# Keys and queries by block products over the whole depth, with raw weights laid out and loaded by block

## The chip, the cores and the metric

The kernel runs on one core of a Trainium2 chip. The metric is the device time of one execution in microseconds (us); lower is better. Times are compared as medians of several executions. A core has TensorE (PE, with its weight loads shown as PEld), VectorE (DVE), ScalarE (ACT), GpSimd (POOL) and SyncE (SP), each with its own queue of instructions in order; DMA transfers are started from SP, ACT and POOL.

## The reference

One inference step of a two-layer trunk on 576 tokens: a prompt of 512 and eight samples of eight. Layer 0 is a gated short convolution; layer 1 is an mLSTM block with four heads of 512. What matters here is how layer 1 gets its keys and queries, and what it does with them:

```python
xm, z = jnp.split(h @ w_in, 2, axis=-1)
xc, new_buf = causal_dwconv(xm, conv_buf, conv_w)
xc = jax.nn.silu(xc + conv_b)
q = xc @ w_q                      # (576 x 2048) @ (2048 x 2048)
k = xc @ w_k
v = xm @ w_v
...
# per head and chunk of 64 tokens (8 for the samples)
S = jnp.einsum('bhid,bhjd->bhij', qj, kj) * jnp.exp(logD - m_row[..., None])
num = w_inter[..., None] * jnp.einsum('bhid,bhde->bhie', qj, C) + jnp.einsum('bhij,bhje->bhie', S, vj)
den = w_inter * jnp.einsum('bhid,bhd->bhi', qj, n) + jnp.sum(S, axis=-1)
C_new = decay[..., None, None] * C + jnp.einsum('bhjd,bhje->bhde', kw, vj)
```

Inputs and outputs are float32. `C` is the matrix memory, given for the eight samples (the old states) and zero for the prompt.

## The kernel before

**Products.** Data lie with features on the 128 partitions and the 576 tokens along the free axis. Each float32 operand is split in a high part, which TensorE takes as it is, and a low rest, and a product is three matmuls: high weight x high data, high x low, low x high. Weights are split in the kernel: `parts_of` copies the raw weights to the high part on ACT (L264) and subtracts on DVE (L265), in tiles of 512 columns (four buffers) or 256 (two buffers). A split tile serves 4 (or 2) blocks of 128 x 128.

**Block products.** Where two k-tiles of the input meet two tiles of the output and the tokens are taken as two halves of 288, `block_pair` (L330) forms a 2 x 2 block product with seven products instead of eight: sums and differences of the data (the "forms", made once by `forms` and kept) meet sums of the weight blocks a11, a12, a21, a22 (made on DVE for each step: L298, L299 and L350). The seven products go to three PSUM banks, called p1, p5 and p6, one after the other: a11, s1, s2, a12, a21, s2 again, a22; results are added up from the banks by ACT and DVE.

**The stage.** Keys and queries are made in 16 steps, heads in the order 3, 0, 1, 2 and four steps to a head. A step makes 128 key rows (`k`) and 128 query rows (`q`) for all tokens, from 16 k-tiles of `xc`, thus eight pairs of k-tiles. Six pairs go by block products (7 x 6 x 3 = 126 matmuls of 288 columns, L345) and the last four k-tiles plainly (`plain`, L433: 4 x 2 outputs x 2 halves x 3 = 48). The very first step, `gemm_first`, does four pairs by block and eight k-tiles plainly, since the forms of pairs 4 and 5 are still in the making. The raw weights of a step are four loads of 512 KB (`wr`, L320, issued by SP), asked for at the end of the step before by `block_weights`, which also makes the sums.

**What runs between.** `run` takes a piece of work from a list at marked places between products: transposes of the finished keys for storage (L768, L769), scores, gates. `drip` takes one from a slower list: `meet` (L909) multiplies a piece of an old state, loaded as two `c` tiles of 512 KB into two buffers, with the queries (`query_state`, L857). After eight pieces of a head the product is copied into a tile `qc`, which stays in one of the slots of 128 x 576 that hold nearly all data (`N_SLOT`, 70 of them) until `sample_numerators` (L1305) uses it, far behind. Only heads 3, 0 and 1 do so here; head 2 follows later.

**The end of the stage.** The last step ends with `next_stage`: it loads layer 1's eight input tiles `x` again, runs what is left in the list, and normalises them for the z branch (`second_norm`: L902 on DVE, then a split of each with L166 on ACT and L167 on DVE). The z tiles follow, with weights from chunk 192 on.

The code is written in the order in which each engine's queue gets its instructions, up to a scheduler that moves instructions a little by their estimated readiness; waits between engines are semaphores. An engine that waits holds all that stands behind it in its queue.

## Time and profile before

| | us |
|---|---|
| median of 3 runs (lowest, highest) | 1635.63 (1635.1, 1638.68) |
| profiled execution, its own time | 1636.74 |
| its span | 1634.9 |
| PE busy | 1610.5 |
| DVE busy | 1117.4 |
| ACT busy | 807.0 |
| stage of keys and queries, steps 2 to 15 | about 839 to 1236 |

The mean granted clock of TensorE in this execution is 0.994 of full speed. The profiled execution's time is its span and 1.84 us around it. Busy time is the union of an engine's instructions; matmuls overlap, so PE at 99% says that some matmul is always in flight. Group rows give line, engine, operation, output<-input, shapes and count, then busy time, mean ns of one, and the idle time of the engine just before them with what ended it. DMA rows give size and the median time from issue to landing.

### The profile page before, as it was taken

How to read it: one execution, taken by the hardware profiler on the slowest of the kernel's cores; microseconds unless marked ns; L12 is line 12 of the kernel's file. 1: busy time of each engine (PE TensorE's matmuls, PEld its weight loads, DVE VectorE, ACT ScalarE, POOL GpSimd, SP SyncE). 2: the span in 40 equal slices, each digit the busy share in tenths (PEclk: the TensorE clock that was granted, in tenths of full speed). 3: DMA queues.
4: the chain of work that ended last, by engine and by line, in shares of the span. 5: the costliest groups of instructions: out<-in, count | busy, mean ns of one | idle time of the engine just before them, and what ended most of it. 6: DMA issues, size and time to landing. Idle time of an engine off the chain costs nothing. (4 is left out here: it accounts for less than half of the span.)

```text
span 1634.9 us, 31031 instructions
## 1 busy us (share of the span) xinstructions
PE 1610.5 (99%) x11981; PEld 1540.3 (94%) x11981; DVE 1117.4 (68%) x2124; ACT 807.0 (49%) x1622; POOL 139.3 (9%) x263
## 2 busy tenths in 40 slices
PE   9999999999999999999999999999999998999998
PEld 9999999999999999999999998999997798999997
DVE  7988988886336985655865555445458578688765
ACT  5566666654233554444644444344345556555421
POOL 1111111110000000000011010010112000000000
PEclk9999999999999999999999999999999999999999
DMA  6477676754332434443533555455467898998992
GB/s 222 110 168 176 167 166 171 168 146 145 122 126 87 144 109 141 128 143 124 181 110 117 171 161 170 157 178 158 156 203 272 293 313 318 342 352 297 359 336 101
DMA packets 118052, 306.85 MB, mean 188 GB/s; under 512 B 12912, under 2 KB 29168, under 8 KB 117904
## 3 DMA queue, kind: packets, MB, share of 16 engines
q1 hardware_dynamic: 94480, 272.86, 50.0%
q0 software_dynamic: 8064, 14.68, 6.0%
q10 hardware_dynamic: 15360, 17.32, 3.1%
q8 instruction: 94, 1.54, 0.4%
q14 instruction: 54, 0.44, 0.1%
HBM read 244.29 MB, written 60.52 MB: 186 GB/s over the span
## 5 line engine op out<-in xcount | busy, mean ns | idle before, releaser
L345 PE MATMUL p<-hi,wh 128*128 128x288 f32 x1540 | 453.7, 296 | 1.7 <-ACT wh L264 1.0
L345 PE MATMUL p<-lo,wh 128*128 128x288 f32 x1540 | 452.6, 295 | 0.0
L345 PE MATMUL p<-hi,wl 128*128 128x288 f32 x1540 | 451.0, 295 | 0.2 <-DVE wl L265 0.2
L345 PEld LDWEIGHTS p<-hi,wh 128*128 128x128 f32 x1540 | 288.3, 188 | 12.8 <-DVE ws L350 6.6
L345 PEld LDWEIGHTS p<-lo,wh 128*128 128x128 f32 x1540 | 289.0, 188 | 0.0
L345 PEld LDWEIGHTS p<-hi,wl 128*128 128x128 f32 x1540 | 288.1, 188 | 0.6 <-DVE wl L265 0.6
L264 ACT CAST wh<-wr 128x512 fp32r<-128x512 f32 x298 | 171.4, 578 | 213.9 <-PE p L345 121.1
L265 DVE TENSOR_TENSOR wl<-wr,wh 128x512 fp32r<-128x512 f32 x298 | 184.9, 634 | 91.7 <-ACT wh L264 90.5
L235 PE MATMUL acc<-hi,wh 128*128 128x256 f32 (+1 forms) x1072 | 232.8, 298 | 2.5 <-ACT num L1302 1.2
L235 PE MATMUL acc<-lo,wh 128*128 128x256 f32 (+1 forms) x1072 | 231.3, 297 | 0.0
L235 PE MATMUL acc<-hi,wl 128*128 128x256 f32 (+1 forms) x1072 | 231.1, 297 | 0.0
L264 ACT CAST wh<-ws 128x512 fp32r<-128x512 f32 (+1 forms) x201 | 114.9, 573 | 195.2 <-PE p L345 121.9
L215 ACT CAST wh<-wr 128x512 fp32r<-128x512 f32 x170 | 105.0, 619 | 197.6 <-PE acc L235 149.5
L235 PEld LDWEIGHTS acc<-hi,wh 128*128 128x128 f32 x1072 | 180.1, 190 | 9.6 <-issue 3.9
L216 DVE TENSOR_TENSOR wl<-wr,wh 128x512 fp32r<-128x512 f32 x170 | 116.4, 688 | 102.4 <-ACT wh L215 90.6
L235 PEld LDWEIGHTS acc<-lo,wh 128*128 128x128 f32 x1072 | 179.8, 190 | 1.8 <-issue 1.7
L235 PEld LDWEIGHTS acc<-hi,wl 128*128 128x128 f32 x1072 | 179.7, 190 | 0.8 <-issue 0.7
L265 DVE TENSOR_TENSOR wl<-ws,wh 128x512 fp32r<-128x512 f32 (+1 forms) x201 | 125.4, 629 | 74.7 <-ACT wh L264 74.2
L433 PE MATMUL p<-hi,wh 128*128 128x288 f32 x496 | 109.2, 300 | 0.0
L433 PE MATMUL p<-hi,wl 128*128 128x288 f32 x496 | 107.8, 295 | 0.0
L433 PE MATMUL p<-lo,wh 128*128 128x288 f32 x496 | 106.6, 295 | 0.0
L1236 DVE SCALAR_TENSOR_TENSOR c<-c,cols,r 128x512 f32<-128x512 f32 x128 | 90.7, 741 | 16.5 <-PE r L1235 13.9
(385 smaller groups left out, 2569.0 us busy)
## 6 DMA issues: line engine op xcount, KB each, us to landing
wr<-wts SPq DMA_DIRECT2D x222, 512.0 KB, 3.6
c<-cs SPq DMA_DIRECT2D x128, 512.0 KB, 6.0
cs_out<-c SPq DMA_DIRECT2D x64, 512.0 KB, 7.0
ws<-wts SPq DMA_DIRECT2D x28, 256.0 KB, 4.3
ws<-wts POOLq DMA_DIRECT2D x28, 256.0 KB, 4.8
wr<-wts POOLq DMA_DIRECT2D x28, 256.0 KB, 4.2
x<-xcs SPq DMA_DIRECT2D x20, 288.0 KB, 4.3
x<-xT SPq DMA_DIRECT2D x16, 288.0 KB, 4.2
```

Source lines behind the costliest of these rows:

```text
L215: last_act[0] = nc.scalar.copy(hi, raw[:, 4 * i:4 * i + 4, :]).ins
L216: nc.vector.tensor_tensor(lo, raw[:, 4 * i:4 * i + 4, :], hi.bitcast(F32), ALU.subtract)
L235: nc.tensor.matmul(acc[:, o:o + j - i], a[:, k % 4, :], x[:, i:j], start=(first and k == 0 and p == 0), stop=(last and k == 7 and p == 2))
L264: last_act[0] = nc.scalar.copy(hi, src).ins
L265: nc.vector.tensor_tensor(lo, src, hi.bitcast(F32), ALU.subtract)
L345: nc.tensor.matmul(bank_, a[:, j, :], x, start=(start and n + j + i == 0), stop=(n == len(groups) - 1 and j == len(g) - 1 and i == 2), ski ...
L433: nc.tensor.matmul(b, a[:, k % 4, :], x[:, t:t + HT], start=bool(start) and k == 0 and i == 0, stop=(k == n - 1 and i == 2), skip_group_ch ...
L1236: ins = nc.vector.scalar_tensor_tensor(ct[:, j, :], ct[:, j, :], dec[:, o + j:o + j + 1], r, ALU.mult, ALU.add).ins
```

## The change

- Steps 0 and 1 multiply as before. While they run, the forms of the last two k-pairs are made too (`mixed_load(6)` and `(7)`), from `xc` tiles loaded again.
- Steps 2 to 15 use a new function `eight_pair`: all eight pairs by block products, 7 x 8 x 3 = 168 matmuls of 288 columns, every weight split 512 columns wide (the 256-wide buffers are gone). Banks and order of the seven products are as before; results go straight to `k` and `q` without the plain part's additions.
- The host lays out these steps' raw weights so that each load of 512 KB holds one block (a11, a12, a21 or a22) of all eight pairs. The loads for the next step are issued inside the step, block by block in the order a11, a21, a22, a12, after products 3, 4, 5 and 7, when the step's own tile comes free. The next step's first sums (a21 + a22, `eight_sums`) stand after product 7.
- `qc` of each head is stored to DRAM from ACT's queue (`qcs`, 128 x 513) and fetched again when that head's numerators are at their second tile. The second norm's row scale `rb` is stored to DRAM too (`rbs`) and loaded again in the last step; the gate weights `wif` move to slots. There are 73 slots.
- The last step spreads its end: `rbs` and the eight `x` loads after product 1, raw weights of z tiles 192 and 193 after products 3 and 4, the second norm two tiles at a time after products 4 to 7.

```diff
@@ 49 -> 49 @@
-N_SLOT = 70
+N_SLOT = 73
@@ 262 -> 262 @@
-            hi, lo = [wpool.tile([P, n, P], F32R, name=f"w{t[0]}{uid[0]}", tag=t if n == 4 else t[0] + "x",
-                                 bufs=4 if n == 4 else 2) for t in ("hi", "lo")]
+            hi, lo = [wpool.tile([P, n, P], F32R, name=f"w{t[0]}{uid[0]}", tag=t, bufs=4) for t in ("hi", "lo")]
@@ 388 -> 387 @@
-                block_weights(*then)
+                if len(then) == 1:
+                    for i in (0, 2, 3, 1):
+                        eight_load(then[0], i)
+                    eight_sums(then[0])
+                else:
+                    block_weights(*then)
@@ 419 -> 424 @@
+        eights = {}
+        def eight_load(c_, i):
+            t = weight_tile()
+            latest[0] = load(out=t, in_=io["wts"][c_ + i]).ins
+            eights.setdefault(c_, {})[i] = t
+        def eight_sums(c_):
+            e = eights[c_]
+            e["s"] = [X(512, name="ws").rearrange("p (k x) -> p k x", x=P) for _ in range(2)]
+            for g in range(2):
+                k = slice(4 * g, 4 * g + 4)
+                nc.vector.tensor_tensor(e["s"][g], e[2][:, k, :], e[3][:, k, :], ALU.add)
+        def eight_pair(c_, fs, out1, out2, then=None, calls={}):
+            e = eights.pop(c_)
+            tt = nc.vector.tensor_tensor
+            o11, o12, o21, o22 = out1[:, 0:HT], out1[:, HT:NT], out2[:, 0:HT], out2[:, HT:NT]
+            a11, a12, a21, a22 = [[e[i][:, 4 * g:4 * g + 4, :] for g in range(2)] for i in range(4)]
+            sums = e["s"]
+            def product(n, bank_, ws, form, start):
+                ws = [parts_of(w) for w in ws]
+                for g, w in enumerate(ws):
+                    for j in range(4):
+                        hi, lo = fs[4 * g + j][form]
+                        for i, (a, x) in enumerate(((w[0], hi), (w[0], lo), (w[1], hi))):
+                            nc.tensor.matmul(bank_, a[:, j, :], x, start=(start and g + j + i == 0),
+                                             stop=(g == 1 and j == 3 and i == 2), skip_group_check=True)
+            def after(n):
+                if n in calls:
+                    calls[n]()
+                run()
+                if n in (4, 6):
+                    drip()
+            bx = block("p1")
+            product(1, bx, a11, "b11", True)
+            by = block("p6")
+            nc.scalar.activation(by, bx, AF.Copy, scale=-1.0)
+            after(1)
+            bw = block("p5")
+            product(2, bw, sums, "t1", True)
+            m5 = X(HT, name="m5")
+            nc.scalar.copy(m5, bw)
+            for g in range(2):
+                tt(sums[g], sums[g], a11[g], ALU.add)
+            after(2)
+            product(3, by, sums, "t2", False)
+            nc.scalar.copy(o12, by)
+            for g in range(2):
+                tt(sums[g], sums[g], a12[g], ALU.add)
+            for g in range(2):
+                tt(a21[g], a21[g], a11[g], ALU.add)
+            if then:
+                eight_load(then, 0)
+            after(3)
+            product(4, bx, a12, "b21", False)
+            nc.scalar.copy(o11, bx)
+            if then:
+                eight_load(then, 2)
+            after(4)
+            product(5, by, a21, "t3", False)
+            tt(o22, by, m5, ALU.subtract)
+            if then:
+                eight_load(then, 3)
+            after(5)
+            product(6, bw, sums, "b22", False)
+            tt(o12, bw, o12, ALU.subtract)
+            after(6)
+            product(7, by, a22, "t4", False)
+            if then:
+                eight_load(then, 1)
+                eight_sums(then)
+            nc.scalar.copy(o21, by)
+            after(7)
@@ 743 -> 829 @@
+        rbs = dram.tile([P, NT], F32, name="rbs")
+        store(out=rbs, in_=rb)
@@ 746 -> 833 @@
-            w = S([P, P], name="wif")
+            w = T(P, name="wif")
@@ 820 -> 907 @@
-        Sc, qcs = {}, {}
+        Sc = {}
+        qcs = [dram.tile([P, 513], F32, name=f"qcs{h}") for h in range(NH)]
@@ 866 -> 954 @@
-                qcs[st["h"]] = qc
+                store_act(out=qcs[st["h"]], in_=qc)
@@ 902 -> 990 @@
-                nc.vector.scalar_tensor_tensor(xs[m], xs[m], col("norm1", m), rb, ALU.mult, ALU.mult)
+                nc.vector.scalar_tensor_tensor(xs[m], xs[m], col("norm1", m), scale[0], ALU.mult, ALU.mult)
@@ 924 -> 1012 @@
-                def next_stage():
-                    for m in range(KD):
+                def next_loads():
+                    for t, src in [(scale, rbs)] + [(xs, x1s[m]) for m in range(KD)]:
@@ 927 -> 1015 @@
-                        load(out=x, in_=x1s[m])
-                        xs.append(x)
-                    run(len(work))
-                    second_norm(range(KD))
+                        load(out=x, in_=src)
+                        t.append(x)
@@ 933 -> 1019 @@
-                    xs = []
-                then = next(((128 + 4 * g, 130 + 4 * g, True) for i, g in enumerate(order) if i and order[i - 1] == f), None)
-                if (h, dt) == (3, 0):
-                    gemm_first(128 + 4 * f, 130 + 4 * f, fc, xc, k, q, [lambda j=j: mixed_load(j) for j in (4, 5)], then)
+                    xs, scale, first_z = [], [], []
+                n = order.index(f)
+                then = 128 + 4 * order[n + 1] if n + 1 < len(order) else None
+                if n == 0:
+                    gemm_first(128 + 4 * f, 130 + 4 * f, fc, xc, k, q, [lambda j=j: mixed_load(j) for j in (4, 5)], (then, then + 2, True))
+                elif n == 1:
+                    work.extend([mixed_load(6), lambda: work.append(mixed_load(7))])
+                    gemm_pair(128 + 4 * f, 130 + 4 * f, fc, xc[4:], k, q, then=(then,), pops=1)
@@ 938 -> 1028 @@
-                    gemm_pair(128 + 4 * f, 130 + 4 * f, fc, xc[4:], k, q, mid=[next_stage] if (h, dt) == (2, 3) else None, then=then, pops=1)
+                    eight_pair(128 + 4 * f, fc, k, q, then, {} if then else {
+                        1: next_loads, 3: lambda: first_z.append(raw_weights(192)),
+                        4: lambda: (first_z.append(raw_weights(193)), second_norm((0, 1))),
+                        5: lambda: second_norm((2, 3)), 6: lambda: second_norm((4, 5)), 7: lambda: (run(len(work)), second_norm((6, 7)))})
@@ 966 -> 1060 @@
+        first_z = [weights(192, raw=raw) for raw in first_z]
@@ 974 -> 1068 @@
-            acc = gemm(192 + f, 1, h2, pops)
+            acc = mm("acc")
+            products(acc, first_z.pop(0) if first_z else weights(192 + f), h2, True, True, pops)
@@ 1307 -> 1402 @@
-            qc = qcs[h]
+            qc, = fetched.pop(("q", h))
@@ 1453 -> 1549 @@
+                if it == 1:
+                    fetch(("q", h), qcs[h], n=513)
@@ 1635 -> 1733 @@
+    even = kq.transpose(0, 1, 3, 2, 4, 5).reshape(NW, 2, P, NW, P)
+    even = np.concatenate([even[:, :, :, 0::2], even[:, :, :, 1::2]], 3)
+    even = even.reshape(NW, 2, P, 2, KD, P).transpose(0, 1, 3, 2, 4, 5)
+    kq = np.concatenate([even[:12], kq[12:14], even[14:]], 0)
```

Over the whole program PE has 84 fewer matmuls of this shape, DVE 21 fewer instructions, ACT 32 fewer, and SP 10 more rows.

Three places show how the order of instructions moves. The first is DVE's queue at the end of a middle step. Here `wl` is the low part of a split weight, `wr` a raw block, `ws` a block sum, `q` the query rows, and a number behind a name tells buffers apart. Before:

```order
L265 TENSOR_TENSOR wl1667_12331<-wr1627_12052,wh1667_12330 128x512
L265 TENSOR_TENSOR wl1663_12281<-wr1631_12060,wh1663_12280 128x256
L265 TENSOR_TENSOR wl1669_12357<-wr1630_12059,wh1669_12356 128x512
L265 TENSOR_TENSOR wl1666_12309<-ws1632_12063,wh1666_12308 128x256
L298 TENSOR_TENSOR ws1673_12368<-wr1672_12365 128x512
L299 TENSOR_TENSOR ws1674_12369<-ws1673_12368,wr1671_12364 128x512
L350 TENSOR_TENSOR wr1672_12365<-wr1672_12365,wr1671_12364 128x4x128
L265 TENSOR_TENSOR wl1670_12361<-wr1631_12060,wh1670_12360 128x512
L265 TENSOR_TENSOR wl1668_12335<-wr1631_12060,wh1668_12334 128x256
L265 TENSOR_TENSOR wl1689_12457<-wr1671_12364,wh1689_12456 128x512
L265 TENSOR_TENSOR wl1690_12461<-wr1675_12372,wh1690_12460 128x256
```

With the change:

```order
L264 TENSOR_TENSOR wl1614_11975<-wr1573_11672,wh1614_11974 128x512
L264 TENSOR_TENSOR wl1615_11979<-wr1573_11672,wh1615_11978 128x512
L264 TENSOR_TENSOR wl1617_12010<-ws1588_11792,wh1617_12009 128x512
L264 TENSOR_TENSOR wl1618_12014<-ws1589_11793,wh1618_12013 128x512
L264 TENSOR_TENSOR wl1622_12051<-wr1579_11715,wh1622_12050 128x512
L438 TENSOR_TENSOR ws1625_12084<-wr1610_11964,wr1616_12007 128x512
L438 TENSOR_TENSOR ws1626_12085<-wr1610_11964,wr1616_12007 128x512
L491 TENSOR_TENSOR q1592_11806<-p61596_11840,m51604_11888 128x288
L481 TENSOR_TENSOR wr1610_11964<-wr1610_11964,wr1607_11929 128x512
L264 TENSOR_TENSOR wl1623_12055<-wr1579_11715,wh1623_12054 128x512
L481 TENSOR_TENSOR wr1610_11964<-wr1610_11964,wr1607_11929 128x512
L264 TENSOR_TENSOR wl1633_12104<-wr1607_11929,wh1633_12103 128x512
```

Before, the next step's sums (L298, L299, L350) stand between splits of the last plain weights. Now the first two rows are splits for product 5 (a21), the next two for product 6, `wl1622` and `wl1623` for product 7; the next step's two sums (L438) and product 5's result (L491) stand between the last two.

The second is SP's queue in the same step: raw weights (L320 before, L429 now), old states (`c`), and a store of transposed keys (`kss`). Before:

```order
L320 DMA wr1626_12051<-wts 128x1024
L178 DMA c1615_11959<-cs 128x1024
L774 DMA kss0_7300<-tb1605_11864 64x128
L178 DMA c1616_11961<-cs 128x1024
L320 DMA wr1627_12052<-wts 128x1024
L320 DMA wr1630_12059<-wts 128x1024
L320 DMA wr1631_12060<-wts 128x1024
L178 DMA c1634_12096<-cs 128x1024
L178 DMA c1635_12098<-cs 128x1024
```

With the change:

```order
L429 DMA wr1607_11929<-wts 128x1024
L861 DMA kss0_7302<-tb1600_11850 64x128
L429 DMA wr1610_11964<-wts 128x1024
L178 DMA c1612_11970<-cs 128x1024
L178 DMA c1613_11972<-cs 128x1024
L429 DMA wr1616_12007<-wts 128x1024
L429 DMA wr1624_12082<-wts 128x1024
L178 DMA c1620_12046<-cs 128x1024
L178 DMA c1621_12048<-cs 128x1024
```

Before, a step's four raw loads stood close together with one pair of states after the first. Now they come one by one, and one pair of states stands between the second and the third.

The third is DVE in the last step. `x` are the second norm's tiles, `x2004` the row scale, `lo` the low part of a normalised tile, `tb` a transposed key. Before:

```order
L902 SCALAR_TENSOR_TENSOR x2085_15120<-x2085_15120,cols_69,rb794_6155 128x576
L265 TENSOR_TENSOR wl2109_15177<-wr2046_14823,wh2109_15176 128x512
L265 TENSOR_TENSOR wl2082_15073<-ws2048_14827,wh2082_15072 128x256
L902 SCALAR_TENSOR_TENSOR x2086_15122<-x2086_15122,cols_69,rb794_6155 128x576
L902 SCALAR_TENSOR_TENSOR x2087_15124<-x2087_15124,cols_69,rb794_6155 128x576
L167 TENSOR_TENSOR lo2094_15138<-x2085_15120,hi2093_15137 128x576
L902 SCALAR_TENSOR_TENSOR x2088_15126<-x2088_15126,cols_69,rb794_6155 128x576
L265 TENSOR_TENSOR wl2110_15181<-wr2047_14824,wh2110_15180 128x512
L902 SCALAR_TENSOR_TENSOR x2089_15128<-x2089_15128,cols_69,rb794_6155 128x576
L167 TENSOR_TENSOR lo2096_15143<-x2086_15122,hi2095_15142 128x576
L902 SCALAR_TENSOR_TENSOR x2090_15130<-x2090_15130,cols_69,rb794_6155 128x576
```

With the change:

```order
L264 TENSOR_TENSOR wl2021_14828<-ws1993_14706,wh2021_14827 128x512
L990 SCALAR_TENSOR_TENSOR x2005_14761<-x2005_14761,cols_69,x2004_14759 128x576
L479 TENSOR_TENSOR ws1993_14706<-ws1993_14706,wr1992_14704 128x512
L859 TENSOR_SCALAR tb2016_14785<-tb2014_14778 64x128
L990 SCALAR_TENSOR_TENSOR x2006_14763<-x2006_14763,cols_69,x2004_14759 128x576
L264 TENSOR_TENSOR wl2022_14832<-ws1994_14707,wh2022_14831 128x512
L990 SCALAR_TENSOR_TENSOR x2007_14765<-x2007_14765,cols_69,x2004_14759 128x576
L990 SCALAR_TENSOR_TENSOR x2008_14767<-x2008_14767,cols_69,x2004_14759 128x576
L479 TENSOR_TENSOR ws1994_14707<-ws1994_14707,wr1992_14704 128x512
L990 SCALAR_TENSOR_TENSOR x2009_14769<-x2009_14769,cols_69,x2004_14759 128x576
L264 TENSOR_TENSOR wl2024_14867<-wr1992_14704,wh2024_14866 128x512
L990 SCALAR_TENSOR_TENSOR x2010_14771<-x2010_14771,cols_69,x2004_14759 128x576
```

Before, the normalising stood behind the last block product's sums, among the splits of the plain part. Now its multiplications stand between the splits for products 3 (`wl2021`, `wl2022`) and 4 (`wl2024`), and the splits of `x` follow further behind.

## The prediction

> **What bounds the kernel now.** I read the page's busy shares first, then the windows around the key and query stage, then the waits of TensorE, and last the timeline of a single step. The page:
>
> ```profile
> PE 1610.5 (99%) x11981; PEld 1540.3 (94%) x11981; DVE 1117.4 (68%) x2124; ACT 807.0 (49%) x1622; POOL 139.3 (9%) x263
> ```
>
> The busy time of PE tells that matmuls are always in flight, so what counts is what one more or one fewer costs, stage by stage. In the windows the columns are length, busy time with instructions of PE, PEld, DVE, ACT and POOL, granted clock, DMA share and GB/s. The first two rows are the stage's first two steps, the third the other fourteen, the fourth the passage to the z tiles, the last all that follows.
>
> ```profile
> 795.00:815.00 20.00, 20.00 (x160) 19.14 (x159) 18.50 (x38) 13.07 (x27) 0.53 (x1) 1.00 0.42 128
> 815.00:839.00 24.00, 23.16 (x175) 22.92 (x174) 18.84 (x41) 13.43 (x30) 3.58 (x5) 1.00 0.38 118
> 839.00:1236.00 397.00, 397.00 (x3002) 366.38 (x3001) 216.31 (x426) 173.37 (x364) 41.52 (x106) 1.00 0.50 160
> 1236.00:1260.00 24.00, 22.96 (x170) 18.36 (x169) 18.72 (x32) 10.99 (x23) 7.48 (x15) 1.00 0.90 313
> 1300.00:1634.00 334.00, 316.76 (x2249) 299.35 (x2249) 250.99 (x504) 165.70 (x355) 12.82 (x29) 0.97 0.86 304
> ```
>
> From 839 to 1236 PE is busy in all of 397 us at the full clock, DVE in 216, ACT in 173, the DMA engines half the time: the fourteen steps that change are bound by TensorE alone. The waits of TensorE over the whole run (what, for whom, us, times, longest) have three near the change, and all are at its edge, in steps 0 and 1 or where the stage ends:
>
> ```profile
> PE ta L768 <- ACT q L415: 1.0, 1, 1.0
> PE p L345 <- ACT wh L264: 1.0, 1, 1.0
> PE p L345 <- ACT m L362: 0.7, 1, 0.7
> ```
>
> So matmuls taken out of steps 2 to 15 come off the end, unless one of the other queues, which the change rearranges, becomes late. **I forecast a gain of about the matmuls removed, less a little at the two ends of the stage.**
>
> **What a matmul costs.** One step on the timeline (start, length, engine, line, what, how many): rows of L345 are block products, those of L433 plain ones.
>
> ```profile
> 838.23 0.42 PE L433 MATMUL p<-hi,wh 128*128 128x288 f32 x2
> ...
> 841.43 0.42 PE L345 MATMUL p<-hl,wh 128*128 128x288 f32 x2
> ...
> 843.81 0.60 PE L768 MATMUL ta<-cst,k 128*128 128x128 f32 x4
> ...
> 844.28 0.38 PE L345 MATMUL p<-hi,wh 128*128 128x288 f32 x1
> 844.49 0.29 PE L345 MATMUL p<-lo,wh 128*128 128x288 f32 x1
> ...
> 856.27 0.42 PE L433 MATMUL p<-hi,wh 128*128 128x288 f32 x2
> ...
> 858.09 0.29 PE L345 MATMUL p<-hi,wh 128*128 128x288 f32 x1
> ...
> 860.50 0.42 PE L433 MATMUL p<-lo,wh 128*128 128x288 f32 x2
> ...
> 864.91 0.42 PE L345 MATMUL p<-hl,wh 128*128 128x288 f32 x2
> ```
>
> The lengths overlap, so I go by starts. Plain: 24 in 3.20 us (838.23 to 841.43), 14 in 1.82, 34 in 4.41: 133, 130 and 130 ns. Block: 89 in 11.78 us (844.49 to 856.27), 18 in 2.41: 132 and 134 ns. The whole step is 23.48 us for 174 matmuls and 0.47 us of transposes: 132 ns each. I take 131 for a plain one and 132.6 for a block one. The Trainium skill's page "TensorE: Matmul & The Clock Gate", section "Back-to-back issue gap", gives N/2.4 + 2.5 ns for an isolated warm matmul; by that, 288 columns take 122.5 ns (an estimate), and the 84 fewer below would be worth 10.3 us. The rows of this stage are 6 to 9% above it, and decide.
>
> **Matmuls, part by part.** Of 16 k-tiles a step multiplied twelve by block products and four plainly: 126 + 48 = 174 matmuls. Steps 2 to 15 now make 7 x 8 x 3 = 168, all block. Per step 48 plain fall away (6.29 us) and 42 block ones come (5.57): 0.72 us less, times 14 is **10.0 us**. With 130 against 133.3 ns and 132 against 134 the ends are 8.5 (plain 130, block 134) and 12.0 (133.3 and 132). The pieces of state products and transposes that are dripped between products are the same in number, and only move.
>
> **DVE and ACT, steady.** Groups by form in 839 to 1236 (busy us, mean ns, then idle before and its releaser):
>
> ```profile
> L265 DVE TENSOR_TENSOR wl<-wr,wh 128x512 fp32r<-128x512 f32 x83 | 57.3, 691 | 67.8 <-ACT wh L264 67.6
> L264 ACT CAST wh<-wr 128x512 fp32r<-128x512 f32 x83 | 51.6, 621 | 107.4 <-PE p L345 52.0 <-PE p L433 46.7 <-ACT q L413 8.6
> L265 DVE TENSOR_TENSOR wl<-wr,wh 128x256 fp32r<-128x256 f32 x55 | 23.0, 419 | 0.0
> L298 DVE TENSOR_TENSOR ws<-wr 128x512 f32<-128x512 f32 x13 | 9.0, 692 | 10.4 <-DMA wr<-wts 10.4
> L298 DVE TENSOR_TENSOR ws<-wr 128x256 f32<-128x256 f32 x13 | 5.5, 426 | 28.0 <-DMA wr<-wts 28.0
> L416 DVE TENSOR_TENSOR q<-p,m 128x288 f32<-128x288 f32 x14 | 6.4, 456 | 23.2 <-PE p L433 23.2
> ```
>
> A step's weight splits were, in the block part, nine of 512 and seven of 256 columns; all fourteen are now of 512: 14 x 0.69 against 9 x 0.69 + 7 x 0.42, +0.5 us. Its block sums were four of each width and are now eight of 512: +1.1. DVE gains 1.6 us a step, 216 + 22 = 239 us of 387, 62%. ACT's casts go with the splits and a copy falls away: unchanged within 0.3 us. Both are hidden behind PE on average: priced at nothing, and if the cover were gone DVE's 22 us would be the bill.
>
> **The chain in the queues.** On average is not enough, since DVE takes its work in order, and the next step's two sums (L438), which wait for raw weights, now stand ahead of product 5's result (L491) and of the second half of product 7's weights. Behind them queue those weights and, on PE, product 7. That DVE can wait for raw weights the L298 rows show already: 38 us in these steps, with no wait of PE behind it. What it costs now depends on how late the load comes:
>
> ```profile
> wr<-wts SPq DMA_DIRECT2D x54, 512.0 KB, 3.5
> c<-cs SPq DMA_DIRECT2D x48, 512.0 KB, 4.9
> x<-x1s SPq DMA_DIRECT2D x8, 288.0 KB, 7.0
> DMA to landing us min/median/max: 3.3/3.5/5.4
> ```
>
> (The fourth row is that of the raw weights in this stage.) A product is 24 x 0.1326 = 3.18 us. From the step's start: product 5's second weights need the buffer that product 3 leaves at 9.5 us; transposes (0.47) and a state product push this to 10.5.
>
> ```profile
> 947.94 1.06 PE L857 MATMUL qa<-c,qp 128*32 128x512 f32 x8
> 878.01 0.69 DVE L350 TENSOR_TENSOR wr<-wr,wr 128x512 f32<-128x512 f32 x1
> 878.62 1.78 DVE L265 TENSOR_TENSOR wl<-wr,wh 128x512 fp32r<-128x512 f32 x3
> ```
>
> The state product is the first row; the other two show DVE operations of this size starting 0.61 us apart. With a cast (0.62) and a split (0.69) the block e3's load is issued at 10.9, as its buffer comes free, or at 12.4 with the transposes and the state product. It lands 3.5 later, up to 2 more if it shares the engines with the two state loads issued just ahead of it: at 14.4 to 17.9. Two sums (1.38) and the result (0.46) then free product 7's bank at 16.2 to 19.7, against a start of product 7 at 19.1 to 20.6; one more sum and the split (1.38) bring the second weights at 17.6 to 21.1, against 20.7 to 22.2, twelve matmuls into the product. That is about 3 us of slack at the usual landing and 1 at the worst; I take 1 off for hand-overs between engines that no row shows, so 2 and 0. Price: nothing, with 0 to 3 us for a few bad steps. State loads, issued after product 6 and used 48 matmuls (6.4 us) later, had 42 matmuls (5.6 us) before, and PE did not wait for them.
>
> **Steps 0 and 1.** They also make the forms of the last two k-pairs, from tiles loaded again. A form is five half-width operations (0.456) and three splits (0.75), 4.5 us by lengths and 3.9 with the overlap of 0.08 each that the starts above show; two are 7.7 us. In 815 to 839 DVE is busy 18.84 of 24, so 5 us are free; from 822.5 the order has 15.9 us of DVE work to come, counted with these durations, which ends at 838.4, and the first product of step 2 needs its forms at 841.4. Bounds: 0 with this 3 us of slack, 3 if the 2.7 us that do not fit into the 5 fall late. I take **+0.5**, near the lower end since the slack is as large as the excess.
>
> **The last step and the passage.** Its queue of DVE now has eight normalising operations between weights, and they wait for nine loads (the row scale and eight x) that SP issues after product 1 and behind state loads.
>
> ```profile
> 1222.70 0.82 DVE L902 SCALAR_TENSOR_TENSOR x<-x,cols,rb 128x576 f32<-128x576 f32 x1 [2.69 <-DMA x<-x1s]
> L902 DVE SCALAR_TENSOR_TENSOR x<-x,cols,rb 128x576 f32<-128x576 f32 x8 | 6.3, 814 | 2.7 <-DMA x<-x1s 2.7
> L167 DVE TENSOR_TENSOR lo<-x,hi 128x576 fp32r<-128x576 f32 x8 | 5.6, 750 | 0.0
> ```
>
> DVE waited 2.69 us for x before, with PE not held up; now the second half of product 3's weights and all of product 4's stand behind that wait. The row scale and first x should land about when DVE arrives, 7 us after issue. If they are 3 us late, PE loses up to 3: the bounds are 0 and 3, I take **+0.7**, as the 2.69 us wait is the nearest row and most of a product's lead covers it. In return the 11.9 us of normalising (6.3 and 5.6) no longer stand at the end, and the 1.04 us that PE idled in 1236 to 1260 can go (0 to -1): **-0.8**.
>
> **The late stage.** The old states' products now come back from DRAM, four loads of 262 KB, and the raw weights of z 192 and 193 come earlier.
>
> ```profile
> DMA packets 41627, 120.33 MB, mean 305 GB/s; under 512 B 4608, under 2 KB 6848, under 8 KB 41591
> wr<-wts SPq DMA_DIRECT2D x29, 512.0 KB, 6.4
> PE num L1289 <- ACT z L986: 3.4, 1, 3.4
> 1300.00:1304.00 4.00, 4.00 (x13) 3.03 (x14) 2.90 (x5) 2.81 (x9) 0.00 (x0) 0.54 0.97 280
> 1304.00:1306.00 2.00, 2.00 (x7) 1.21 (x5) 1.93 (x4) 2.00 (x7) 0.00 (x0) 0.50 1.05 425
> 1306.00:1308.00 2.00, 1.99 (x9) 1.46 (x9) 2.00 (x5) 0.51 (x1) 0.00 (x0) 0.71 1.03 420
> ```
>
> From 1240 on 120.33 MB move at 305 GB/s; 1.05 MB more is 3.4 us of transfer time at that rate, at a DMA share of 0.86, spread over four heads, on queues whose work PE seldom waits for. "DMA: Bandwidth & Descriptors" of the Trainium skill, section "Where 436 GB/s comes from", puts a core's share of HBM at about 358 GB/s; by it the 120.33 MB fill 336 of the 394 us and the extra 2.9 us fit in (an estimate). The rows of 425 and 420 GB/s are above that figure, over 4 us. Bounds: 0, if PE's own work covers the loads, and 3.4 if it all comes out at the end; I take **+0.6**, near the lower end, as PE waits in this stage sum to a few us only. The last three rows also show a clock of 0.54, 0.50 and 0.71 over 8 us; if the shifted order spares that, 1.8 + 1.0 + 0.6 = 3.4 us are won. I do not count on it.
>
> **The sum.** -10.0 + 0.5 + 0.7 - 0.8 + 0.6 = -9.0. From the profiled execution, 1636.74 us (span 1634.9 and 1.84 around it), -9.0 gives 1627.7. That execution stands 1.1 above the median 1635.63, so on the median about 1626.6; I say **1626.5**.
>
> **The rivals.** (a) The gain is mostly eaten at the two ends: steps 0 and 1 cost 3, the last step 3, no idle time is won, and the late loads cost 1: -10.0 + 7 = -3.0, about 1632.6, nearly no change. For it: DVE's 18.84 of 24 us and the x wait; against it, the slack worked out. (b) Slower: **each step's product 7 waits for the next step's raw weights**, through DVE's order. It begins at landings of 5.5 us (3.5 and 2 of slack), and costs 1 us a boundary for each us beyond, at 13 boundaries. The 9.0 us are eaten at 6.2, and with landings at 6.5 13 us go: 1635.6 - 9.0 + 13 = 1639.6. For it: 6.4 us is the median of the same loads in the late stage; against it, that stage has a DMA share of 0.86, this one 0.50, and the largest landing here is 5.4. (c) Faster than I say: the idle time at the passage and the slow clock after 1300 both go, -9.0 - 0.2 - 3.4, and with the matmuls at their upper end 2.0 more: 1635.6 - 14.6 = 1621. (d) That the change does not do what it says can be left out: the order shows 84 fewer matmuls of this shape.
>
> **How the numbers follow.** Forecast 0.69, with a range of its own of 1622 to 1631 (8.5 to 12.0 for the matmuls, the ends at 0 to 4); (a) 0.15, (b) 0.08, (c) 0.08. The range 1620 to 1634 holds the forecast, most of (a) and half of (c). Within 0.2%, 3.3 us, a measurement of this kernel cannot tell a change. Faster, below 1632.4: forecast 0.68, (c) 0.08, and 0.05 of (a), 0.81; same 0.11; slower 0.08.
>
> **What would show it.** Right: PE starts in steps 2 to 15 still 131 to 133 ns apart with no wait, the stage 9 to 11 us shorter from its first to its last product, DVE near 62% there. Wrong: a wait of PE on L491 or on weights at product 7, in every step (b); PE waits between 830 and 842, or in the last step for weights behind L990 (a); new waits on the fetched query products after 1300. A stage 10 us shorter and an end that is not would show a late stage bound by its loads.

## The result, and the profile after

The changed kernel takes 1642.42 us (median of 6 runs, 1639.77 to 1643.96) against 1636.5 for the kernel before (6 runs): a ratio of 1.0035, 95% interval 1.0025 to 1.0045. It is 5.9 us slower, where 10 us faster was forecast. The page of the profiled execution:

```profile
span 1640.5 us, 30832 instructions
PE 1607.8 (98%) x11897; PEld 1533.9 (94%) x11897; DVE 1159.1 (71%) x2112; ACT 811.4 (49%) x1586; POOL 149.7 (9%) x263
```

PE is busy 2.7 us less and the span is 5.6 us longer. The window of the fourteen changed steps at the same place as before (length, busy time with instructions of PE, PEld, DVE, ACT and POOL, granted clock, DMA share, GB/s):

```profile
839.00:1236.00 397.00, 393.72 (x2952) 359.85 (x2951) 254.70 (x411) 178.79 (x334) 54.02 (x121) 1.00 0.50 163
```

TensorE is idle there for 3.3 us, where it was busy throughout before: 1.8 on old states, 0.6 on weights in the last step, and 0.9 at the passage to the z tiles, which now lies in this window. Five of the waits of TensorE over the whole run (for whom, on whom: us, times, longest):

```profile
PE r L1330 <- DVE c L1331: 4.7, 14, 1.5
PE num L1384 <- ACT z L1081: 3.3, 1, 3.3
PE acc L235 <- ACT num L1397: 2.1, 2, 1.9
PE qa L945 <- DMA c<-cs: 1.8, 3, 1.1
PE num L1384 <- DVE ld L1499: 1.6, 1, 1.6
```

All but the fourth lie behind the stage that was changed. The timeline tells where the time goes. After (start, length, engine, line, what, how many, and the idle time before it with its cause): step 2 begins, the last product ends, the first z tile begins, a z matmul behind all work left over from the stage, and one near the end.

```profile
840.79 0.42 PE L454 MATMUL p<-hl,wh 128*128 128x288 f32 x2
...
1231.04 0.29 PE L454 MATMUL p<-hi,wl 128*128 128x288 f32 x1
1232.20 0.66 PE L855 MATMUL ta<-cst,k 128*128 128x128 f32 x4 [0.88 <-ACT q L502]
...
1232.73 0.51 PE L235 MATMUL acc<-hi,wh 128*128 128x256 f32 x2
...
1273.77 0.43 PE L235 MATMUL acc<-hi,wh 128*128 128x256 f32 x2
...
1572.90 0.43 PE L235 MATMUL acc<-hi,wh 128*128 128x320 f32 x2
```

The same two last matmuls in the kernel before (matched by their count from the end):

```profile
1281.40 0.39 PE L235 MATMUL acc<-hi,wh 128*128 128x256 f32 x1
...
1567.42 0.43 PE L235 MATMUL acc<-hi,wh 128*128 128x320 f32 x2
```

So the changed kernel is **7.6 us ahead** when the stage and its leftovers are done (1273.77 against 1281.40), and **5.5 us behind** 300 us later (1572.90 against 1567.42): the late stage, in whose code the change puts only the trip of the query products, loses 13 us. Windows between the same z matmuls tell where, before and after (the second of three stretches, which lasts 142 us in both, is left out):

```profile
1281.40:1340.80 59.40, 58.76 (x388) 51.70 (x385) 43.42 (x92) 34.65 (x78) 4.17 (x8) 0.94 0.88 295
1483.34:1506.20 22.86, 20.84 (x148) 19.01 (x146) 22.23 (x38) 11.16 (x20) 0.90 (x3) 1.00 0.70 236
```

```profile
1273.77:1339.32 65.55, 63.09 (x393) 54.15 (x392) 43.85 (x92) 35.86 (x80) 2.99 (x10) 0.90 0.83 288
1481.50:1511.69 30.19, 24.22 (x150) 21.56 (x148) 22.65 (x38) 13.49 (x23) 0.97 (x3) 0.89 0.70 230
```

The first stretch, right behind the stage, loses 6.2 us, and the third, around the last head's numerators, 7.3. TensorE in the third, before and after:

```profile
1495.76 0.50 PE L1235 MATMUL r<-vst,km 128*128 128x512 f32 x1 [0.73 <-DVE c L1236]
1496.42 0.49 PE L1235 MATMUL r<-vst,km 128*128 128x512 f32 x1 [0.16 <-DVE c L1236]
1497.09 0.39 PE L1289 MATMUL num<-vh,hi 128*128 128x256 f32 x1 [0.17 <-DVE ld L1404]
1497.31 0.28 PE L1290 MATMUL num<-vh,hi 128*128 128x258 f32 x1
1497.43 0.28 PE L1289 MATMUL num<-vh,lo 128*128 128x256 f32 x1
...
1498.62 0.39 PE L1235 MATMUL r<-vst,km 128*128 128x512 f32 x1
```

```profile
1495.13 0.39 PE L1384 MATMUL num<-vh,hi 128*128 128x256 f32 x1 [1.64 <-DVE ld L1499]
...
1496.67 0.39 PE L1330 MATMUL r<-vst,km 128*128 128x512 f32 x1
1497.71 0.49 PE L1330 MATMUL r<-vst,km 128*128 128x512 f32 x1 [0.65 <-DVE c L1331]
1498.37 0.49 PE L1330 MATMUL r<-vst,km 128*128 128x512 f32 x1 [0.16 <-DVE c L1331]
1499.03 0.50 PE L1330 MATMUL r<-vst,km 128*128 128x512 f32 x1 [0.16 <-DVE c L1331]
1501.03 1.46 PE L1330 MATMUL r<-vst,km 128*128 128x512 f32 x2 [1.49 <-DVE c L1331]
1502.28 0.41 PE L1384 MATMUL num<-vh,hi 128*128 128x256 f32 x1
1502.49 0.42 PE L1385 MATMUL num<-vh,hi 128*128 128x258 f32 x1
```

The numerators at 1497.09 before are those at 1495.13 after. Before, one update of new states (`r`) stands between them and the next group, at 1498.62; now six do, and TensorE waits four times for DVE's part of them (`c`, L1331). And from 1502 on the numerators start 0.21 us apart, where before it was 0.12 (1497.31 to 1497.43): the clock has halved. The window around 1500 of the changed kernel shows it; before, the clock there was full.

```profile
1500.00:1510.00 10.00, 8.80 (x45) 8.04 (x45) 6.21 (x11) 1.65 (x3) 0.37 (x2) 0.66 0.88 304
```

Summed over windows of 10 us from 1230 to 1630, the missing share of the clock is 8.5 us before and 15.3 after. By that, about half of the 13 us is slow clock behind a gap and not the gap itself (an estimate, as it counts the slow clock in waits too). The page "TensorE: Matmul & The Clock Gate" of the Trainium skill, section "Part 1: The HAM clock gate", has two clocks in its table of states, full and half, and the half one after an idle window of some 3.4 us; the trace agrees with the two clocks (starts 0.21 against 0.12 us apart; 0.66 over 10 us is half clock for 6.8 of them), but here the fall came behind waits of 0.2 to 1.6 us each. A little later DVE and ACT of the changed kernel stand:

```profile
1511.10 0.49 DVE L1405 TENSOR_SCALAR ld<-ld,cols 128x513 f32<-128x513 f32 x1 [4.89 <-DMA ld<-qcs]
1510.44 0.72 ACT L1233 ACTIVATE ld<-ld,cols 128x512 f32<-128x512 f32 x1 [8.39 <-DMA ld<-kss]
```

The first is the scaling of the fetched query products, the second that of stacked key rows, for which ACT waited before the change as well (5.51 us at this place). These two waits were the first suspects; the experiments bear neither out.

### The profile page after: what moved, and what is told of

Read it like the earlier page. It is cut to its first block, busy times and chain, and to the rows that moved or that the text cites. A ratio compares the mean times of both kernels' runs of the same rounds, so it can differ in the third digit from the quotient of the medians.

```text
span 1640.5 us, 30832 instructions
## 1 busy us (share of the span) xinstructions
PE 1607.8 (98%) x11897; PEld 1533.9 (94%) x11897; DVE 1159.1 (71%) x2112; ACT 811.4 (49%) x1586; POOL 149.7 (9%) x263
## 4 chain that ended last, share of the span: by engine, by line
PE 61%; DVE 3%; DMA 3%; ACT 1%; issue 1%; POOL 0%; SPq 0%; DVEq 0%; ACTq 0%; POOLq 0%
PE p L454 17%; PE acc L235 16%; PE p L344 7%; PE p L518 7%; PE qa L945 2%; PE cp L1384 2%; PE cp L1385 1%; PE r L1330 1%; DVE c L1331 1%; PE ta L855 1%; PE g L838 1%; DMA c<-cs 1%; PE s L964 1%; PE blk L518 1%; DMA ld<-kss 1%
## 5 line engine op out<-in xcount | busy, mean ns | idle before, releaser
L344 PE MATMUL p<-hi,wh 128*128 128x288 f32 x1036 | 305.4, 295 | 2.6 <-ACT wh L263 1.0
L344 PE MATMUL p<-lo,wh 128*128 128x288 f32 x1036 | 304.5, 294 | 0.0
L344 PE MATMUL p<-hi,wl 128*128 128x288 f32 x1036 | 302.7, 295 | 0.2 <-DVE wl L264 0.2
L263 ACT CAST wh<-wr 128x512 fp32r<-128x512 f32 (+1 forms) x270 | 166.0, 617 | 216.1 <-PE p L454 112.0
L264 DVE TENSOR_TENSOR wl<-wr,wh 128x512 fp32r<-128x512 f32 (+1 forms) x270 | 184.8, 687 | 81.2 <-ACT wh L263 79.5
L215 ACT CAST wh<-wr 128x512 fp32r<-128x512 f32 x170 | 105.0, 619 | 196.5 <-PE acc L235 140.8
L454 PE MATMUL p<-hi,wh 128*128 128x288 f32 x672 | 201.3, 300 | 0.0
L454 PE MATMUL p<-hi,wl 128*128 128x288 f32 x672 | 199.2, 297 | 0.6 <-DVE wl L264 0.6
L344 PEld LDWEIGHTS p<-hi,wh 128*128 128x128 f32 x1036 | 194.3, 188 | 4.2 <-ACT wh L263 1.2
L454 PE MATMUL p<-lo,wh 128*128 128x288 f32 x672 | 197.8, 294 | 0.0
L344 PEld LDWEIGHTS p<-lo,wh 128*128 128x128 f32 x1036 | 194.4, 188 | 0.0
L216 DVE TENSOR_TENSOR wl<-wr,wh 128x512 fp32r<-128x512 f32 x170 | 116.6, 687 | 110.0 <-ACT wh L215 102.8
L344 PEld LDWEIGHTS p<-hi,wl 128*128 128x128 f32 x1036 | 193.4, 188 | 0.4 <-DVE wl L264 0.4
L454 PEld LDWEIGHTS p<-hi,wh 128*128 128x128 f32 x672 | 126.1, 188 | 12.5 <-ACT wh L263 2.5
```

The lines of the kernel that those rows point to most:

```text
L215: last_act[0] = nc.scalar.copy(hi, raw[:, 4 * i:4 * i + 4, :]).ins
L216: nc.vector.tensor_tensor(lo, raw[:, 4 * i:4 * i + 4, :], hi.bitcast(F32), ALU.subtract)
L263: last_act[0] = nc.scalar.copy(hi, src).ins
L264: nc.vector.tensor_tensor(lo, src, hi.bitcast(F32), ALU.subtract)
L344: nc.tensor.matmul(bank_, a[:, j, :], x, start=(start and n + j + i == 0), stop=(n == len(groups) - 1 and j == len(g) - 1 and i == 2), ski ...
L454: nc.tensor.matmul(bank_, a[:, j, :], x, start=(start and g + j + i == 0), stop=(g == 1 and j == 3 and i == 2), skip_group_check=True)
```

## The experiments

In all ratios the divisor is the kernel before, run beside it on the same chip; its medians were 1636.3 to 1636.8 us, so that medians can be compared too, within a few tenths.

| run | median, us | ratio (95%) |
|---|---|---|
| the change | 1642.4 | 1.0035 (1.0025 to 1.0045) |
| fewer | 1632.4 | 0.9979 (0.9968 to 0.9990) |
| trip | 1655.0 | 1.0108 (1.0094 to 1.0122) |
| early | 1642.3 | 1.0032 (1.0020 to 1.0044) |
| nospread | 1647.1 | 1.0077 (1.0064 to 1.0090) |
| idletrip | 1641.5 | 1.0029 (1.0017 to 1.0041) |
| qpool | 1641.0 | 1.0030 (1.0020 to 1.0040) |
| qkspool | 1642.4 | 1.0029 (1.0013 to 1.0045) |
| kspool | 1640.6 | 1.0027 (1.0017 to 1.0036) |
| notrip | 1642.0 | 1.0035 (1.0022 to 1.0049) |
| nowait | 1640.6 | 1.0024 (1.0014 to 1.0035) |
| half | 1653.6 | 1.0108 (1.0093 to 1.0124) |
| halffewer | 1643.1 | 1.0040 (1.0028 to 1.0051) |
| fewerpin | 1626.6 | 0.9940 (0.9928 to 0.9952) |
| trippin | 1641.7 | 1.0031 (1.0020 to 1.0042) |
| afterpin | 1634.5 | 0.9991 (0.9983 to 1.0000) |
| earlypin | 1636.9 | 1.0001 (0.9990 to 1.0013) |
| earlypoolpin | 1634.7 | 0.9988 (0.9979 to 0.9998) |
| kept2pin | 1632.4 | 0.9974 (0.9963 to 0.9984) |

### First: is it the earlier arrival, the trip, or the spreading?

**fewer**: the kernel before without 84 of its plain matmuls.

```diff
+                        if short[0] and i == 1 and (k, t) in ((1, 0), (1, HT), (2, 0)):
+                            continue
                         nc.tensor.matmul(b, a[:, k % 4, :], x[:, t:t + HT], ...
```

> The kernel before with nothing changed but that each of steps 2 to 15 leaves out 6 of its 48 plain matmuls (high weights x low data of three half tiles of each output), so 84 matmuls of 288 columns less, the number the change saves; the output lacks these terms. Theory A (the late stage passes nothing on: its flow of old states sets the end, and arriving earlier only means waiting): of the 84 x 0.131 = 11.0 us at most 4 arrive at the end, 1632 to 1636. Theory B (the late stage passes the gain on, and the change's own additions lost it there): 8 to 11 us arrive, about 1626.

Only 3.4 us arrive by the ratio (4.1 by the medians). That is what theory A wanted. Its twelve runs spread over 10.3 us (1628.27 to 1638.53), those of the kernel before beside it over 3.7; the profiled one is the slowest.

**trip**: the kernel before with the store and the fetch of the query products alone.

```diff
-                qcs[st["h"]] = qc
+                store_act(out=qcs[st["h"]], in_=qc)
 ...
                 numerators(h, it)
+                if it == 1:
+                    fetch(("q", h), qcs[h], n=513)
```

> The kernel before with one part of the change alone: the old states' query products of the four heads stored to DRAM from ACT's queue and fetched again at each head's second numerators. Theory B with the fetch as the culprit (DVE waited 4.89 us for the last fetch, and the state updates behind it): 5 to 9 us slower than before, 1641 to 1645, with a wait of DVE on the fetch at the last head. Theory A: the bytes alone, 0 to 3 us slower.

18.5 us slower, where theory B had 5 to 9 for the wait and theory A 0 to 3 for the bytes. DVE's two waits for the fetches are 8.3 us there, the longer one 6.3.

That seemed to settle on the trip. **early** moves two fetches ahead in the changed kernel, and **nospread** takes the spreading of the last step back:

```diff
-                if it == 1:
+                if it == 1 and h in (1, 2):
                     fetch(("q", h), qcs[h], n=513)
 ...
+        fetch(("q", 0), qcs[0], n=513)
 ...
+            if h == 2:
+                fetch(("q", 3), qcs[3], n=513)
```

> The changed kernel with the fetches for the first and last head asked for earlier (the first ahead of the last z tile before the numerators, the last ahead of that head's keys), the bytes the same. If the late fetch is the culprit: the 4.89 us wait of DVE goes and 4 to 8 us are won, 1634 to 1638. If the bytes or the earlier arrival are: no change, 1641 to 1643.

```diff
-                    eight_pair(..., {1: next_loads, 3: ..., 4: ..., 5: ..., 6: ..., 7: ...})
+                    eight_pair(..., {7: lambda: (next_loads(), run(len(work)), second_norm(range(KD)))})
```

> The changed kernel with the last step's spreading undone: the loads of x, the list of pieces and the whole second norm again at the step's end, the first z weights where they were. If the spreading lost the time (pieces and z weights out of step with the late stage): 3 to 8 us faster, 1634 to 1639. If not: 0 to 4 slower, since the normalising stands at the end again.

In **early** DVE's wait for the fetches is down to 0.8 us, and the time is the same; another wait has grown instead, ACT's for the stacked key rows (in the changed kernel 13.7 in all, the longest 8.4):

```profile
DVE ld L1405 <- DMA ld<-qcs: 0.8, 1, 0.8
ACT ld L1233 <- DMA ld<-kss: 19.3, 4, 10.5
```

**nospread** is 4.7 us slower than the change (6.9 by the ratios): the spreading is not the culprit.

### Second: the wait, or the place in SP's queue?

**idletrip** makes the trip but computes with the tile on the chip; **qpool** issues the fetches from POOL's queue; **qkspool** those of the key rows too; **kspool** the key rows alone, in the kernel before.

```diff
-            qc, = fetched.pop(("q", h))
+            fetched.pop(("q", h))
+            qc = st["qc"]
```

> The kernel before with the query products stored and fetched as in the run of the trip alone (1655.0), but the numerators use the tile that stayed on the chip, so no engine waits for a fetch. If DVE's wait for the fetched tile is what the trip costs (8.3 us of waits there, and the half clock behind): most of the 18.5 us goes, 1637 to 1642. If the four fetches cost by standing in SP's queue among the loads and stores of old states (which ACT's wait for the key rows, kss, shows): 1648 to 1655.

```diff
-                    fetch(("q", h), qcs[h], n=513)
+                    fetch(("q", h), qcs[h], n=513, load=add_load)
```

Here `add_load` is `nc.gpsimd.dma_start`, and `fetch` gets the new argument.

> The changed kernel with one edit: the four fetches of query products are issued from POOL's queue instead of SP's, at the same place of the program, bytes the same. If their place in SP's queue is what costs (SP then reaches the key rows and states sooner): 3 to 8 us faster than the changed kernel, 1634 to 1639. If bytes or the wait of DVE cost: within 2 us of 1642.

The other edit, in qkspool beside that one and in kspool alone:

```diff
-                    fetch(("ks", *j), copies(kss[j[0]], j[1]))
+                    fetch(("ks", *j), copies(kss[j[0]], j[1]), load=add_load)
```

> The same, and the loads of the stacked key rows (kss), for which ACT stands 13.7 us in the changed kernel with its copies out of the numerators' banks behind, from POOL's queue too. If SP's order is the limit at the last head: ACT's wait of 8.4 us near 1510 falls below 2, the half clock there goes, and 8 to 14 us are won against the changed kernel, 1628 to 1634, faster than before. If DMA flow is the limit: 1640 or more.

> The kernel before with the loads of the stacked key rows alone moved to POOL's queue. ACT waits 16.4 us for them there, the longest 6.0. If SP's order holds back this stage before the change too: 3 to 6 us faster than before, 1630 to 1633. If flow: no change.

Only idletrip came as the wait theory had it (4.8 slower than before, not 18.5). The two runs on the changed kernel gain nothing that can be told, though in **qkspool** ACT no longer waits for key rows at all; it waits for raw weights (from 1230 on; 16.2 us in the changed kernel):

```profile
ACT wh L215 <- DMA wr<-wts: 19.5, 7, 4.6
```

And **kspool**, which takes away a wait of 16.4 us (0.6 is left), makes the kernel before 4.4 us slower, where 3 to 6 us faster or no change was expected. Except in idletrip, no removed wait came off the end.

### Third: taking work out of the late stage

**notrip** leaves store and fetch away, **nowait** only the reading (both lack the old states' share of the samples' output); **half** lets each store of a new state write half its bytes, **halffewer** leaves out the 84 matmuls too.

```diff
-            qc, = fetched.pop(("q", h))
-            nc.vector.tensor_scalar(qc, qc, ...
+            qc = T(513, name="ld")
+            nc.vector.tensor_scalar(qc, st["nums"][0][:, 0:513], ...
```

> The changed kernel without the trip: query products are neither stored nor fetched, and the four scalings that need them take a tile that is on the chip anyway, so the samples' output lacks the old states' share. Every engine's instructions are as many, 2.1 MB of transfers less. If the trip is what ate the gain: 1624 to 1631 (10 to 18 us faster than the changed kernel, since the trip alone cost 18.5 before and its mere transfers 4.8). If the late stage absorbs whatever comes earlier: 1634 to 1640.

> The changed kernel with the query products stored and fetched as ever, but nobody reads what is fetched (the scalings take a tile on the chip, the samples' output lacks the old states' share). It lies between the changed kernel and the run without the trip: what separates it from the first is DVE's wait for the fetches, what separates it from the second the transfers and their place in SP's queue. By the trip on the kernel before (13.5 us wait, 4.8 transfers): 1630 to 1636, nearer to the run without the trip. If waits are only swapped for others: within 2 us of the changed kernel.

```diff
-  store(out=cs_out[...][:, 2 * (n % 2):2 * (n % 2) + 2], in_=t)
+  store(out=cs_out[...][:, 2 * (n % 2):2 * (n % 2) + 1], in_=t[:, 0:1])
```

> The kernel before with each of the 64 stores of new states writing half its bytes (256 KB instead of 512; half of the state output is missing): 16.8 MB of 120 MB less in the late stage. If that stage is set by the flow of transfers (DMA share 0.86 to 1.0, six buffers that wait for their stores): 10 us or more faster, 1615 to 1627, and the waits for kss and states shrink. If by PE and DVE: 0 to 4 us faster.

> The same with the 84 matmuls left out as well. If the flow of transfers is what absorbed 7 of their 11 us: now 9 to 11 us come off against the kernel with half stores. If something else absorbs them (half clock, DVE's updates): again about 4.

All theories fall here. Without the trip the changed kernel is as slow as with it (1642.0), so with the scheduler's own order it is not the trip that costs. In notrip's trace the two z matmuls of the result stand at

```profile
1271.76 0.43 PE L235 MATMUL acc<-hi,wh 128*128 128x256 f32 x2
...
1573.15 0.43 PE L235 MATMUL acc<-hi,wh 128*128 128x320 f32 x2
```

that is 9.6 us ahead of the kernel before (1281.40) and then 5.7 behind (1567.42): 15 us lost in the late stage without any trip. With 16.8 MB less to store, the kernel before is 17.2 us slower, where it would be 10 or more faster if the flow of transfers set this stage. And on top of that the 84 matmuls are worth 10.5 us, though alone they were worth 4; the flow would explain that, had its first half not just failed. A kernel that gets slower by doing less is not bound by what it does. What all these kernels share is that the scheduler, which sets the order of instructions by its own estimate of times, set another order for the late stage. In the traces, of the last 2700 rows of PE, 560 of DVE, 420 of ACT and 330 of SP of the kernel before, so many would have to be taken out for the rest to stand in the same order in both (names and shapes compared without buffer numbers, so a move among rows of one name does not show; the last three kernels follow below):

```
            PE   DVE  ACT  SP
the change  138   54   22   42
fewer        84   30    9   17
trip         91   48   17   27
half         21   41   13   34
kspool       41   28    7   24
notrip      152   61   24   47
fewerpin      1    0    0    0
trippin       0    4    0    4
afterpin      4    4    3   19
```

### Fourth: the order held fast

For **theory C**, that the order eats the gain, each engine's queue was held in the order that it has in the kernel before, by edges of order between neighbours in a queue. They make no engine wait for an end; they only forbid the scheduler to swap. What is left for trippin and afterpin in the table lies in the trip and, for afterpin, at the end of the key and query stage, whose code differs.

```diff
+def keep_order(tc, table):
 ...
+        for a, b in zip(names, names[1:]):
+            tc.add_manual_dep(have[b], a, mybir.DependencyInfo(mybir.DependencyClass.NoSync, mybir.DependencyReason.DATA),
+                              reason="keep_order")
 ...
         trunk(tc, args)
+        keep_order(tc, ORDER_TABLE)
```

**fewerpin** is fewer, **trippin** trip and **afterpin** the changed kernel, so held: the first two in the whole program, the third from the end of the key and query stage on. The trip's stores, fetches and scalings, which the kernel before does not have or has elsewhere, keep the scheduler's place between them.

> The kernel before without the 84 matmuls of the earlier run (1632.4 there), but with every engine's queue held in exactly the order of the kernel before, by edges of order alone that make nobody wait for an end. Theory C (the scheduler's new order of the late stage ate the gain): 9 to 11 us faster than before, 1625 to 1628. Theory A (an earlier arrival is absorbed): 1631 to 1634, as without the pinned order.

> The kernel before with the trip of the query products alone (1655.0), in the order of the kernel before on all engines, but for the four stores, the four fetches and the scalings that follow them. Theory C: nearly all of the 18.5 us goes, 1636 to 1642. Theory B (the trip itself costs, by waits of DVE and SP): 1648 or more.

> The changed kernel with its late stage (all that is written behind the last step of keys and queries) in the order of the kernel before on each engine, but for the trip's fetches and scalings. It reached the late stage 7.6 us ahead. Theory C: 5 to 10 us faster than before, 1627 to 1632. Theories A and B: 1638 or more.

Two of the three fell as theory C said. The 84 matmuls are worth 10.2 us by the medians (9.8 by the ratio) instead of 4, and the trip costs 5 us instead of 18.5. The changed kernel is 8.0 us faster with the old order (7.2 by the ratios), but at 1634.5 it missed the 1627 to 1632 that theory C gave it: it still pays for the trip. In the profiled execution of fewerpin, the two z matmuls of the result, the windows that hold the last head's numerators, which stand some 13 us earlier here, and ACT's waits for the key rows are:

```profile
1270.66 0.54 PE L237 MATMUL acc<-hi,wh 128*128 128x256 f32 x2
...
1557.83 0.43 PE L237 MATMUL acc<-hi,wh 128*128 128x320 f32 x2
```

```profile
1480.00:1490.00 10.00, 8.57 (x58) 7.21 (x57) 10.00 (x16) 2.21 (x4) 0.37 (x2) 1.00 0.62 204
1490.00:1500.00 10.00, 6.82 (x39) 6.45 (x38) 6.08 (x17) 4.02 (x11) 0.37 (x2) 0.83 1.00 344
```

```profile
ACT ld L1146 <- DMA ld<-kss: 16.6, 4, 7.7
```

fewerpin arrives 10.7 us ahead of the kernel before (1270.66 against 1281.40) and is still 9.6 ahead at the second matmul (1557.83 against 1567.42): an early arrival is passed on. The clock is full through the numerators; it falls only behind them (0.83 over 10 us), and by the windows of 10 us from 1230 to 1630 the missing share of the clock is 6.3 us, against 15.3 in the changed kernel. ACT's wait for key rows is at full length (16.6 us) in the fastest of all runs, so that wait was no cause. Its six runs spread over 3.4 us, where fewer's spread over 10.3; but the other pinned kernels spread over 5.8 to 9.1, so a held order does not make the times steady by itself.

### Last: what is left of the trip, and a kernel that beats both

In the pinned order DVE still waits for two fetches in afterpin (its profiled execution is the slowest of twelve, 1640.0 us):

```profile
DVE ld L1407 <- DMA ld<-qcs: 7.1, 2, 4.4
```

**earlypin** and **earlypoolpin** ask for the same two fetches earlier, as early did, and the second issues all four from POOL; these waits fall to 0.7 and 2.5 us. **kept2pin** is earlypin with head 2's product, which is made behind the stage, left on the chip.

```diff
-                store_act(out=qcs[st["h"]], in_=qc)
+                if st["h"] == 2:
+                    fetched["q", 2] = [qc]
+                else:
+                    store_act(out=qcs[st["h"]], in_=qc)
 ...
-                if it == 1:
+                if it == 1 and h == 1:
                     fetch(("q", h), qcs[h], n=513)
```

> The changed kernel with the late stage in the order of the kernel before, and the fetches of the first and last head's query products asked for earlier, as in the run without the pinned order that gained nothing (1642.3). If DVE's two waits for fetches (2.70 and 4.41 us with the pinned order) are the trip's cost: 3 to 6 us below 1634.5, 1628 to 1632. If the place in SP's queue or the bytes: 1633 to 1636.

> The same with all four fetches issued from POOL's queue, so that none stands among SP's loads and stores of states. If the place in SP's queue costs on top of the waits: 1 to 3 us below the run with early fetches. If only the waits cost: within 1 us of it.

> The run with early fetches from SP's queue and pinned order, but the last-made product, that of head 2, stays on the chip: one store and one fetch less. If the bytes of the late stage cost: 1 to 2 us below the run with early fetches. If not: within 1 us.

Early fetches gain nothing in this order either: earlypin is 2.5 us above afterpin, and earlypoolpin 2.2 below earlypin, with intervals that overlap. One trip fewer, **kept2pin**, is worth 4.6 us against earlypin, more than expected, and makes the fastest kernel with the whole result: 1632.4 us, ratio 0.9974 (0.9963 to 0.9984), faster than both the kernel before and the change.

## Why the prediction was wrong

- **The matmuls, -10.0**: right in size. 84 matmuls less in unchanged queues are worth 10.2 us (fewerpin, which leaves out plain ones). But the sign that was named for it, a stage 9 to 11 us shorter from its first to its last product, did not come: it took 390.2 us (840.79 to 1231.04) against 395.8 before (841.43 to the second matmul of the row at 1237.07), 5.5 less. Summed from start to start in the two traces, the products with their hand-overs took 9.2 us less, the pieces between them 1.3 more, and waits of TensorE added 2.4, the 1.8 and 0.6 of the next two points.
- **The chain in the queues of a middle step, 0**: right. DVE waits for the next step's raw weights as thought, and PE hardly ever for DVE; waits of DVE, and of PE, in steps 2 to 15 of the changed kernel:

```profile
DVE ws L438 <- DMA wr<-wts: 8.5, 13, 1.4
DVE x L990 <- DMA x<-x1s: 3.7, 1, 3.7
PE p L454 <- DVE wl L264: 0.6, 2, 0.4
```

  0.65 us of wait at each of 13 steps, none of which reaches PE, but for 0.6 in the last step, where weights stand among the normalising of x (the second row). Rival (b) did not come about, and DVE is busy 64% there (254.70 of 397), against 62%.
- **State products, nothing**: a small miss. PE waited three times for an old state, 1.8 us (the fourth row of the waits above). These loads were used 6.5 to 7.8 us after issue, no sooner than the soonest before (5.8), but they landed 5.6 to 7.7 us after issue, where those landed after 4.0 to 4.9. The longest wait, 1.05 us, is in the last step, where the nine loads of `x` and the row scale are issued right behind a pair of states; that these held the states up is likely, but no run shows it.
- **Steps 0 and 1, +0.5**: below the bounds of 0 and 3. Step 2 begins 0.6 us earlier, at 840.79.
- **The last step and the passage, +0.7 - 0.8**: the last step's 0.6 us on weights is as it was taken. In the passage TensorE is still idle for 0.88 us, against 1.04. That it is about 1.5 us shorter, twice what was taken, is mostly luck: 1.1 us of gate products moved from there behind the first z matmul.
- Together -9.6 were forecast at the end of the stage, and -7.6 are there.
- **The late stage, +0.6 (0 to 3.4)**: this is the step that failed. It was priced as 1.05 MB of transfers, with everything else as before. It measured +13. That a shifted order changes this stage was thought of only as a gain of 3.4 us, which was not counted; a loss by it was put at nothing without a reason. The ground given for the low price, that the waits of PE in this stage "sum to a few us only", was a misreading too: from 1300 on they sum to 11.4 us, and the window row shows 17 of 334 us idle. The pinned runs give 7 to 8 of the 13 us to the order (1642.4 against 1634.5) and about 5 to the trip (trippin against before). The sum then closes: -9.8 for the matmuls, +5.1 for the trip, +2 for what the stage fell short of its forecast is -2.7; afterpin measured -1.5 by the ratio, with an interval of -2.8 to 0. In the scheduler's own order the two do not add: there the trip's removal won nothing (notrip).
- **The rivals**: the slower one named the wrong queue, and none had the order of a stage behind the change as its mechanism. The last sign, that a shorter stage with an end that is not "would show a late stage bound by its loads", came half and misleads: fewerpin has the same loads and passes its lead on. A range drawn from durations could not hold the result.

What stays open: whether the edges do anything but hold the order (no run holds the kernel before in its own order, or any kernel in a third one); which of the moved rows do the harm (the six state updates ahead of the numerators are one place where it is seen, not a shown cause); what of the trip's 5 us is wait, queue or bytes, as the early fetches gained nothing while one trip fewer gained 4.6; and whether the changed kernel's own best order would beat that of the kernel before, which was only borrowed.

## What to carry to other kernels

Where a scheduler sets the order from its own estimates, an edit can reshuffle the stages that it does not touch: compare the order of the whole program, and give a stage whose rows move a range of its own, up or down, by what such moves have cost. An experiment that takes one thing away means little until the order is held; the same edit was worth 4.1 us with a new order and 10.2 with the old one. When taking away a wait moves the time nowhere and another wait grows, stop chasing waits and ask what else all the variants share.

## What was not expected of the hardware

Halving the stores of new states (16.8 MB less) made the kernel 17 us slower, and moving loads off a queue for which ACT waited 16.4 us made it 4.4 us slower; both with another order of instructions, so they say nothing against the transfers as such. And the granted clock multiplies a poor order: it fell to half behind a series of waits of 0.2 to 1.6 us, and about 7 of the 13 us lost in the late stage are missing clock (15.3 against 8.5 us). It does not explain all of these kernels: kspool misses 5.1 us by the same sum, less than the kernel before, and is 4.4 us slower.
